# Branch gates of a hybrid mixer: eleven of twelve 256-column gate products of a Trainium2 encoder kernel made from seven half-size products

## The chip, the core and the metric

The kernel runs on one core of one Trainium2 chip. The metric is the device time of one execution in microseconds (us). A core has five engines with queues of their own: PE (TensorE, matrix products; PEld is its weight load), DVE (VectorE), ACT (ScalarE), POOL (GpSimd) and SP (SyncE, which issues the loads here). Each takes its instructions in the order of its queue and waits on semaphores for the others. Products are accumulated in PSUM, everything else lies in SBUF.

## The reference

One layer of an encoder over 512 positions of width 1024: a mixer with three gated branches, a cross attention into 256 memory tokens, a gated feed-forward block, and a last norm, all in fp32. The part that is changed is the end of the mixer:

```
p = h @ w_in                                   # h: 512 x 1024, norm of x
...                                            # ya, yb, yc: 512 x 512 each, from p's first columns
br_d = jnp.einsum("bsnc,ncd->bsnd", br, w_branch)     # br = [ya, yb, yc]
g = jax.nn.sigmoid(gates.reshape(bsz, seq, N_BRANCHES, D_MODEL))   # gates: p's last 3 x 1024 columns
merged = jnp.sum(g * br_d, axis=2)
return merged @ w_out
```

So for each of three branches there are a gate product (512 x 1024 by 1024 x 1024) and a branch product (512 x 512 by 512 x 1024).

## The kernel before

**Numbers.** Every fp32 operand of a product is cut into a part hi in the format fp32r (a cast on ACT) and a rest lo = x - hi (a subtraction on DVE); `split` (L101 to L109) and `cut` do both. A product is three accumulated ones: hi by hi, hi by lo, lo by hi. Activations are kept transposed, 128 channels on the partitions by 512 positions, as pairs: hT (the normed input, 8 blocks of 128 channels), ya, yb, yc (4 blocks each), mt (the merged sum, 8 blocks).

**Weights.** `load_raw` (L111) brings 1 MB of weights on SP's queue into one of three buffers (tag wr). `cut` makes pairs of 128 x 1024 elements from it in tags wh and wl, six buffers each (WB). `bank` (L86) hands out four PSUM banks in turn in this stage; the tag acc has four more.

**The gate stage (L660 to L692).** For each branch (yc, yb, ya, in this order) and each block d of 128 output channels, `col_gemm` makes the gate product (L674: 8 channel blocks by 3, so 24 matmuls that stream 512 columns), ACT takes the sigmoid out of PSUM (L676), `gemm` makes the branch product (L680: 12 matmuls of 512 columns), and DVE multiplies both (L683, L685). From the second branch on POOL adds the result to merged (L686); in the third branch `split` then cuts merged into mt (L688). Here Tile, the scheduler that orders the queues, is free: nothing is pinned. It takes instructions by the order of the program among those that its own timing has ready, so later work can fill an engine that it holds to be idle.

**Seven products (L225 to L348).** The feed-forward block already makes its products by Strassen-like sums: a product of (1024 x 256 weights) with (1024 x 512 activations), seen as 2 x 2 blocks, costs seven half-size block products in place of eight. The class `Seven` holds one such item: `sums` (two POOL operations, L242, L243) and `sums2` (two DVE operations, L248, L249) build the weights' sums, `hi` (ACT, L259) and `lo` (DVE, L264) cut them, `mul` (L272) makes one of the seven products (12 matmuls of 256 columns), `keep` (ACT, L278) copies an unfinished sum out of PSUM. The right factors are r11, r21, r22 (quarters of the activations) and t1 to t4 (their sums), which are made once. `seven_run` (L297) writes the order of one period out by hand: the products of item n, the last ones of its predecessor p, and the preparing of its successor q are interleaved:

```
PE:   l11 n, s1 n, s4 p, s2 n, l22 p, l12 n, s3 n
ACT:  u3 p, hi y n, m1 n, gate22 p, hi x q, hi s1 q, u2 n, done0 p, hi b q, c21 p
DVE:  c22 p, lo y n, lo x q, c12 p, sums2 q, lo s1 q, lo b q, c11 n
POOL: sums q
```

Here u3, m1 and u2 are the copies by `keep`; c11, c12, c22 are additions of a copy to what stands in PSUM (DVE, L942 in the feed-forward block); gate22, done0 and c21 finish an item. Each of these instructions is passed to `pin` (L225), which puts it behind the instruction that was written just before it for the same engine, whether that one is pinned or not. `seven_open` (L291) prepares the first item.

The feed-forward block uses this for its last 20 items (L989 to L999), with an item pair of gate and up product per 256 columns; its first 256 columns are made by `col_gemm` (L909 to L919).

**What follows the gate stage.** `Back` (L698) multiplies mt by w_out: `half0` goes through mt's blocks two by two for each of four row tiles (6 matmuls of 512 columns per step), with accumulators of the tag acc.

Of the kernel before, what the change touches and what calls it, by code (L numbers as in the profile page):

```python
# [8 lines left out]
F32 = mybir.dt.float32  # L9
# [8 lines left out]
def encoder_kernel(  # L18
# [39 lines left out]
    def close(p):  # L58
        p_close.pop(id(p))()
# [37 lines left out]
    def nm(s):  # L97
        uid[0] += 1
        return f"{s}{uid[0]}"

    def split(src, hi, lo, scale=None):  # L101

        if scale is None:
            nc.scalar.copy(out=hi, in_=src)  # L104
            nc.vector.tensor_tensor(out=lo, in0=src, in1=hi, op=ALU.subtract)  # L105
# [27 lines left out]
    def gemm(dst, lh, ll, rh, rl, ks, first=True, last=True):  # L133

        n, tot = 0, 3 * len(ks)
        for a, b in ((lh, rh), (lh, rl), (ll, rh)):
            for i, j in ks:
                nc.tensor.matmul(dst, a(i), b(j), start=first and n == 0, stop=last and n == tot - 1)  # L138
# [88 lines left out]
    class Seven:  # L227


        def __init__(self, src, fp, rights, tile_a):  # L230
            self.src, self.fp, self.r, self.tile_a = src, fp, rights, tile_a
            self.l = {}
# [41 lines left out]
                    n += 1  # L274

        def keep(self, name):
            m = self.fp.tile([P, 256], F32, name=nm(name), tag=name, bufs=1)
            pin(nc.scalar.copy(out=m, in_=self.a[:, 0:256]))  # L278
            return m

        def prepare(self):
# [6 lines left out]
            b = self.hi(("s2", "s4"), self.left)  # L288
            self.lo(b)

    def seven_open(items):  # L291
        items[0].load()
        items[0].sums()
        items[1].load()
        items[0].prepare()

    def seven_run(items):  # L297

        z = len(items)
        for k in range(z + 1):  # L300
            n = items[k] if k < z else None
            p = items[k - 1] if k else None
            q = items[k + 1] if k + 1 < z else None
            if k + 2 < z:
                items[k + 2].load()
            if n:
                n.a, n.c = n.tile_a(), n.tile_a()
                n.mul(n.a, "l11", "r11", True, False)
            if p:
# [24 lines left out]
            if p:  # L334
                p.done0()
                p.mul(p.a, "l22", "t4", False, True)
            if q:
                b = q.hi(("s2", "s4"), q.left)
            if p:
                p.c21(p.a[:, 0:256])  # L340
            if n:
                bk = bank(nm("pfb"))
                n.mul(bk, "l12", "r21", True, True)
            if q:
                q.lo(b)
            if n:
                n.c11(bk[:, 0:256], n.m1)
                n.mul(n.a, "s3", "t3", False, False)  # L348


    hp = pool("hp")
# [312 lines left out]
    for n, (b, y) in enumerate(((2, yc), (1, yb), (0, ya))):  # L664
        for half in range(2):
            gts = []
            for c in range(2):
                gts += w_cols(w_in, 8 * W + b * D + half * 512 + c * 256)
                if c == 0:
                    raw = load_raw(w_branch[b, :, half * 512:half * 512 + 512].rearrange("(k p) n -> p k n", p=P), CT, 512)  # L670
                for j in range(2):
                    d = 4 * half + 2 * c + j
                    pgt = bank(nm("pgt"))
                    col_gemm(pgt, gts[2 * c + j], hT, ALLT)  # L674
                    sg = gp.tile([P, T], F32, name=nm("sg"), tag="sg", bufs=3)
                    nc.scalar.activation(out=sg, in_=pgt, func=AF.Sigmoid)  # L676
                    if j == 0:
                        wb = cut(raw, (slice(None), slice(None), slice(c * 256, (c + 1) * 256)), CT, 256)
                    pbr = bank(nm("pbr"))
                    gemm(pbr, lambda i: wb[0][:, i, j * P:(j + 1) * P], lambda i: wb[1][:, i, j * P:(j + 1) * P],  # L680
                         lambda i: y[0][:, i, :], lambda i: y[1][:, i, :], [(i, i) for i in range(CT)])
                    if n == 0:
                        nc.vector.tensor_tensor(out=merged[:, d, :], in0=pbr, in1=sg, op=ALU.mult)  # L683
                    else:
                        nc.vector.tensor_tensor(out=sg, in0=pbr, in1=sg, op=ALU.mult)  # L685
                        nc.gpsimd.tensor_tensor(out=merged[:, d, :], in0=merged[:, d, :], in1=sg, op=ALU.add)  # L686
                        if n == 2:
                            split(merged[:, d, :], mt_[0][:, d, :], mt_[1][:, d, :])  # L688
    close(gp)
    close(yb_p)  # L690
    close(yp)
    close(hp)  # L692

# [210 lines left out]

    HT = (slice(0, T // 2), slice(T // 2, T))
    acc = lambda: psm.tile([P, 512], F32, name=nm("pf"), tag="acc", bufs=4)
    first = []  # L909
    for w in (w_gate_ffn, w_up_ffn):  # L910
        tiles = w_cols(w, 0)
# [24 lines left out]
    class Gate(Seven):  # L936
# [4 lines left out]
        def add(self, o, p, q):  # L941
            pin(nc.vector.tensor_tensor(out=o, in0=p, in1=q, op=ALU.add))  # L942
# [136 lines left out]
```

## Time and profile before

| | |
|---|---|
| median of three runs | 987.66 us (986.48 to 988.14) |
| the profiled execution's own time | 987.72 us |
| its span, first to last instruction | 986.0 us |
| mean granted TensorE clock | 0.994 |
| busy: PE, DVE, ACT, POOL | 964.4, 567.0, 433.2, 182.5 us |
| gate stage, 230.7 to 427.1 us | 196.4 us, PE busy 196.4 |
| seven products of the feed-forward block, 661.6 to 857.4 us | 195.8 us, PE busy 192.8 |

How to read it: the page gives each engine's busy time over the whole span; a row of a timeline gives start, length, engine, line of the kernel, operation, tiles written and read, shapes and count, and in brackets how long the engine sat idle before it and who released it. A row of the lines view gives a group with its busy time and the mean length of one in ns. A row of the windows view gives the busy time of each engine in a stretch, with the granted clock after PEclk.

### The profile page before, as it was taken

Reading aid. Unit: us, or ns where it says so; the run is one execution under the profiler, and the core shown is the slowest. Engines: PE = TensorE matmul, PEld = TensorE weight load, DVE = VectorE, ACT = ScalarE, POOL = GpSimd, SP = SyncE. Lnnn points to the kernel's source line nnn. Section 1 sums busy time; section 2 is a strip of 40 time slices with the busy share of each in tenths; the row PEclk is TensorE's granted clock in tenths of the full one; section 3 lists DMA queues with packets and bytes.
Section 4 is the critical chain, followed back from the end, with each engine's and each line's share of the span. In section 5 each row is a group of like instructions: output and inputs, shape, how many; then the busy total and the mean of one; then the engine's idle time right before and its main releaser. Section 6 shows DMA issues by size and latency. Waiting matters only on the chain. (4 is left out here: it accounts for less than half of the span.)

```text
span 986.0 us, 13484 instructions
## 1 busy us (share of the span) xinstructions
PE 964.4 (98%) x5546; PEld 847.5 (86%) x5546; DVE 567.0 (57%) x719; ACT 433.2 (44%) x652; POOL 182.5 (19%) x175
## 2 busy tenths in 40 slices
PE   7999999999999999999999999999999999899997
PEld 7988888887888888888988888899999999888885
DVE  6686888535323233436845545588888888762313
ACT  6464755334222223335735434554555555641301
POOL 1221123220001121220000000034454545100000
PEclk9999999999999999999999999999999999999999
DMA  9322222222313241362444121204233332532102
GB/s 296 132 86 71 70 74 89 73 86 86 128 43 128 87 128 44 133 211 81 172 153 146 55 74 44 66 21 129 89 126 112 104 128 87 187 107 93 63 1 85
DMA packets 77341, 100.76 MB, mean 102 GB/s; under 512 B 1904, under 2 KB 57248, under 8 KB 77280
## 3 DMA queue, kind: packets, MB, share of 16 engines
q1 hardware_dynamic: 76032, 95.45, 29.1%
q0 software_dynamic: 1248, 4.46, 1.2%
q8 instruction: 43, 0.70, 0.3%
q14 instruction: 18, 0.15, 0.0%
HBM read 97.80 MB, written 2.10 MB: 101 GB/s over the span
## 5 line engine op out<-in xcount | busy, mean ns | idle before, releaser
L105 DVE TENSOR_TENSOR wl<-wr,wh 128x1024 fp32r<-128x1024 f32 x134 | 164.8, 1236 | 204.6 <-ACT wh L104 129.8
L104 ACT CAST wh<-wr 128x1024 fp32r<-128x1024 f32 x134 | 139.8, 1051 | 224.1 <-PE pgt L138 81.1
L264 DVE TENSOR_TENSOR wl<-wr,wh 128x1024 fp32r<-128x1024 f32 x60 | 86.5, 1449 | 21.8 <-ACT wh L259 21.8
L166 POOL TENSOR_TENSOR rs<-ve,mhalf 128x1 f32<-128x1 f32 x22 | 16.0, 729 | 364.9 <-DVE ve L164 364.9
L259 ACT CAST wh<-wr 128x1024 fp32r<-128x1024 f32 x60 | 62.9, 1051 | 13.2 <-DVE wr L249 13.2
L686 POOL TENSOR_TENSOR merged<-merged,sg 128x512 f32<-128x512 f32 x16 | 27.7, 1728 | 184.4 <-DVE sg L685 184.4
L138 PE MATMUL pb<-wh,aTh 128*128 128x512 f32 x176 | 54.3, 390 | 1.7 <-ACT aTh L104 1.7
L138 PE MATMUL pb<-wl,aTh 128*128 128x512 f32 x176 | 54.3, 389 | 0.0
L138 PE MATMUL pb<-wh,aTl 128*128 128x512 f32 x176 | 53.7, 389 | 0.0
L138 PE MATMUL pgt<-hTh,wh 128*128 128x512 f32 x192 | 47.6, 390 | 1.1 <-DVE ybl L105 1.1
L138 PE MATMUL pgt<-hTl,wh 128*128 128x512 f32 x192 | 47.4, 389 | 0.0
L138 PE MATMUL pgt<-hTh,wl 128*128 128x512 f32 x192 | 47.4, 389 | 0.0
L278 ACT COPY u<-pf 128x256 f32<-128x256 f32 x40 | 14.9, 373 | 73.6 <-PE pf L272 71.2
L138 PEld LDWEIGHTS pgt<-hTh,wh 128*128 128x128 f32 x192 | 36.0, 188 | 8.7 <-DVE ybl L105 1.3
L243 POOL TENSOR_TENSOR wr<-wr 128x512 f32<-128x512 f32 x20 | 42.9, 2143 | 1.6
L138 PEld LDWEIGHTS pgt<-hTl,wh 128*128 128x128 f32 x192 | 36.0, 188 | 7.5
L138 PEld LDWEIGHTS pgt<-hTh,wl 128*128 128x128 f32 x192 | 36.0, 188 | 7.5
L138 PEld LDWEIGHTS pb<-wh,aTh 128*128 128x128 f32 x176 | 33.0, 188 | 8.7 <-ACT aTh L104 1.9
L242 POOL TENSOR_TENSOR s<-wr 128x512 f32<-128x512 f32 x20 | 26.1, 1304 | 72.2 <-DVE w L264 69.9
L138 PEld LDWEIGHTS pb<-wl,aTh 128*128 128x128 f32 x176 | 33.0, 188 | 6.9
L138 PEld LDWEIGHTS pb<-wh,aTl 128*128 128x128 f32 x176 | 33.0, 188 | 6.8
L544 POOL TENSOR_SCALAR_AFFINE_SELECT ab<-ab 128x128 f32<-128x128 f32 x32 | 23.8, 780 | 80.1 <-ACT ab L541 80.1
(271 smaller groups left out, 2205.5 us busy)
## 6 DMA issues: line engine op xcount, KB each, us to landing
wr<-in_w_in_dram SPq DMA_DIRECT2D x26, 1024.0 KB, 5.1
wr<-in_w_gate_ffn_dram SPq DMA_DIRECT2D x11, 1024.0 KB, 5.2
wr<-in_w_up_ffn_dram SPq DMA_DIRECT2D x11, 1024.0 KB, 5.6
wr<-in_w_down_ffn_dram SPq DMA_DIRECT2D x10, 1024.0 KB, 4.9
wr<-in_w_branch_dram SPq DMA_DIRECT2D x6, 1024.0 KB, 4.9
wr<-in_w_out_dram SPq DMA_DIRECT2D x4, 1024.0 KB, 5.0
wr<-in_w_k_xa_dram SPq DMA_DIRECT2D x4, 1024.0 KB
wr<-in_w_v_xa_dram SPq DMA_DIRECT2D x4, 1024.0 KB, 5.2
```

The lines of the kernel that those rows point to most:

```text
L104: nc.scalar.copy(out=hi, in_=src)
L105: nc.vector.tensor_tensor(out=lo, in0=src, in1=hi, op=ALU.subtract)
L138: nc.tensor.matmul(dst, a(i), b(j), start=first and n == 0, stop=last and n == tot - 1)
L166: nc.gpsimd.tensor_tensor(out=rs, in0=ve, in1=mhalf, op=ALU.pow)
L242: pin(nc.gpsimd.tensor_tensor(out=self.s1, in0=r[:, 0:4, P:256], in1=r[:, 4:8, P:256], op=ALU.add))
L243: pin(nc.gpsimd.tensor_tensor(out=r[:, 0:4, P:256], in0=r[:, 0:4, 0:P], in1=r[:, 0:4, P:256], op=ALU.subtract))
L259: pin(nc.scalar.copy(out=t[0], in_=src))
L264: pin(nc.vector.tensor_tensor(out=l, in0=src, in1=h, op=ALU.subtract))
L278: pin(nc.scalar.copy(out=m, in_=self.a[:, 0:256]))
L544: nc.gpsimd.affine_select(out=dg, in_=dg, compare_op=ALU.is_gt, fill=0.0, base=0, channel_multiplier=1, pattern=[[-1, P]])
L686: nc.gpsimd.tensor_tensor(out=merged[:, d, :], in0=merged[:, d, :], in1=sg, op=ALU.add)
```

## The change

The gates of eleven of the twelve items (an item is 256 gate columns of one branch) are made from seven half-size products. The first item keeps `col_gemm`; while it runs, the right factors t1 to t4 are made for the whole stage: hT's hi and lo are added again on POOL (8 operations on 128 x 512), the four sums are taken on DVE (16 operations on 128 x 256), and four `split`s cut them into the new pair hTt. The sums use the three weight buffers of the tag wr.

A new class `Branch` adds to `Seven` the branch product of its own 256 columns: `extra_load` brings 0.5 MB of w_branch into one buffer, `extra_cut` cuts it (ACT, DVE), `extra_mul` makes 24 matmuls of 512 columns and then multiplies, adds and splits as before. In `seven_run` the branch product of p comes after the last product of n. Multiplications and additions are pinned; the `split` of merged in the third branch is not, but it is written between pinned ones.

yc and yb move into pools on the right side, and mt takes their place once their last readers are through (from the ninth period on). The copies u3 and m1 now share one buffer (tag m) instead of one each, in the feed-forward block as well.

```diff
-            m = self.fp.tile([P, 256], F32, name=nm(name), tag=name, bufs=1)
+            m = self.fp.tile([P, 256], F32, name=nm(name), tag="u2" if name == "u2" else "m", bufs=1)
...
+            if k == at:
+                got = then()
             if k + 2 < z:
                 items[k + 2].load()
+            if n:
+                n.extra_load()
...
+            if p:
+                p.extra_cut()
             if n:
                 n.c11(bk[:, 0:256], n.m1)
                 n.mul(n.a, "s3", "t3", False, False)
+            if p:
+                p.extra_mul()
...
-    yc = tuple(yp.tile([P, CT, T], F32R, name=f"yc{s}") for s in "hl")
+    ycp = pool("ycp", side="right")
+    yc = tuple(ycp.tile([P, CT, T], F32R, name=f"yc{s}") for s in "hl")
...
-    yb_p = pool("ybp")
+    yb_p = pool("ybp", side="right")
...
-    mtp = pool("mtp", side="right")
-    mt_ = tuple(mtp.tile([P, KD, T], F32R, name=f"mt{s}") for s in "hl")
+    tp = pool("tp")
+    tp.tile([P, 48], F32, name="tpad")
+    hTt = tuple(tp.tile([P, 4, 4, T // 2], F32R, name=f"hTt{s}") for s in "hl")
...
+    gate2 = lambda: gp.tile([P, 2, T], F32, name=nm("sg"), tag="sg", bufs=2)
+    acc = lambda: psm.tile([P, 512], F32, name=nm("pf"), tag="acc", bufs=4)
+    class Branch(Seven):
...
+        def extra_load(self):
+            self.wraw = gp.tile([P, CT, 256], F32, name=nm("wb"), tag="wb", bufs=1)
+            nc.sync.dma_start(out=self.wraw, in_=self.wsrc)
+
+        def extra_cut(self):
+            t = [wp.tile([P, CT, 256], F32R, name=nm(f"w{s}"), tag=f"w{s}", bufs=WB) for s in "hl"]
+            pin(nc.scalar.copy(out=t[0], in_=self.wraw))
+            pin(nc.vector.tensor_tensor(out=t[1], in0=self.wraw, in1=t[0], op=ALU.subtract))
+            self.wb = t
+
+        def extra_mul(self):
+            y = self.y
+            for j in range(2):
+                d = self.d + j
+                pbr = bank(nm("pbr"))
+                m = 0
+                for w, v in ((0, 0), (0, 1), (1, 0)):
+                    for i in range(CT):
+                        pin(nc.tensor.matmul(pbr, self.wb[w][:, i, j * P:(j + 1) * P], y[v][:, i, :],
+                                             start=m == 0, stop=m == 3 * CT - 1))
+                        m += 1
+                sg = self.g[:, j, :]
+                if self.n == 0:
+                    pin(nc.vector.tensor_tensor(out=merged[:, d, :], in0=pbr, in1=sg, op=ALU.mult))
+                else:
+                    pin(nc.vector.tensor_tensor(out=sg, in0=pbr, in1=sg, op=ALU.mult))
+                    pin(nc.gpsimd.tensor_tensor(out=merged[:, d, :], in0=merged[:, d, :], in1=sg, op=ALU.add))
+                    if self.n == 2:
+                        split(merged[:, d, :], mt_[0][:, d, :], mt_[1][:, d, :])
...
+    it = Branch(0, 0)
+    it.extra_load()
+    gts = w_cols(w_in, 8 * W + BR[0][0] * D)
+    it.g = gate2()
+    for j in range(2):
+        pgt = bank(nm("pgt"))
+        col_gemm(pgt, gts[j], hT, ALLT)
+        nc.scalar.activation(out=it.g[:, j, :], in_=pgt, func=AF.Sigmoid)
+    for k in range(4):
+        f = wp.tile([P, 8, T // 2], F32, name=nm("wr"), tag="wr", bufs=3)
+        r11, r12, r21, r22, t1, t2, t3, t4 = (f[:, i, :] for i in range(8))
+        for i, kk in ((0, k), (2, k + 4)):
+            nc.gpsimd.tensor_tensor(out=f[:, i:i + 2, :], in0=hT[0][:, kk, :].rearrange("p (a b) -> p a b", a=2),
+                                    in1=hT[1][:, kk, :].rearrange("p (a b) -> p a b", a=2), op=ALU.add)
+        for o, a, b in ((t1, r12, r11), (t3, r22, r12), (t2, r22, t1), (t4, r21, t2)):
+            nc.vector.tensor_tensor(out=o, in0=a, in1=b, op=ALU.subtract)
+        split(f[:, 4:8, :], hTt[0][:, :, k, :], hTt[1][:, :, k, :])
+    it.extra_cut()
+    items = [Branch(n, c) for n in range(3) for c in range(4)][1:]
+    seven_open(items)
+    it.extra_mul()
...
+    def mt_open():
+        close(yb_p)
+        close(ycp)
+        p = pool("mtp", side="right")
+        mt_.extend(p.tile([P, KD, T], F32R, name=f"mt{s}") for s in "hl")
+        return p
+
+    mtp = seven_run(items, at=8, then=mt_open)
+    mt_ = tuple(mt_)
```

In `Branch` the methods c11, c22 and c12 are DVE additions into the gate's tile g, and gate22, done0 and c21 are sigmoids on ACT.

More of the change, by code (lines that the diff above doesn't have):

```diff
@@ L289, in prepare @@
             self.lo(b)
+        def extra_load(self):
+            pass
+        extra_cut = extra_mul = extra_load
     def seven_open(items):
@@ L295, in seven_open, with seven_run @@
         items[0].prepare()
-    def seven_run(items):
+    def seven_run(items, at=None, then=None):
         z = len(items)
@@ L348, in seven_run @@
                 n.mul(n.a, "s3", "t3", False, False)
+            if p:
+                p.extra_mul()
+        return got if then else None
     hp = pool("hp")
@@ L657, in encoder_kernel @@
     close(up)
-    mtp = pool("mtp", side="right")
-    mt_ = tuple(mtp.tile([P, KD, T], F32R, name=f"mt{s}") for s in "hl")
+    HT = (slice(0, T // 2), slice(T // 2, T))
+    tp = pool("tp")
+    tp.tile([P, 48], F32, name="tpad")
+    hTt = tuple(tp.tile([P, 4, 4, T // 2], F32R, name=f"hTt{s}") for s in "hl")
     gp = pool("gp")
     merged = gp.tile([P, KD, T], F32, name="merged")
[L664 to L688, printed above, removed]
@@ new lines, in encoder_kernel, with __init__, add, sig @@
+    gate2 = lambda: gp.tile([P, 2, T], F32, name=nm("sg"), tag="sg", bufs=2)
+    acc = lambda: psm.tile([P, 512], F32, name=nm("pf"), tag="acc", bufs=4)
+    BR = ((2, yc), (1, yb), (0, ya))
+    mt_ = []
+    class Branch(Seven):
+        def __init__(self, n, c):
+            b, self.y = BR[n]
+            c0 = 8 * W + b * D + c * 256
+            super().__init__(w_in[:, c0:c0 + 256], gp, rights, acc)
+            self.n, self.d = n, 2 * c
+            self.wsrc = w_branch[b, :, c * 256:(c + 1) * 256].rearrange("(k p) n -> p k n", p=P)
+        def add(self, o, p, q):
+            pin(nc.vector.tensor_tensor(out=o, in0=p, in1=q, op=ALU.add))
+        def sig(self, o, i):
+            pin(nc.scalar.activation(out=o, in_=i, func=AF.Sigmoid))
+        def c11(self, p, m):
+            self.g = gate2()
+            self.add(self.g[:, 0, HT[0]], p, m)
+        def c22(self, p, m):
+            self.add(self.g[:, 1, HT[1]], p, m)
+        def gate22(self):
+            self.sig(self.g[:, 1, HT[1]], self.g[:, 1, HT[1]])
+        def c12(self, p, m):
+            self.add(self.g[:, 0, HT[1]], p, m)
+        def done0(self):
+            self.sig(self.g[:, 0, :], self.g[:, 0, :])
+        def c21(self, p):
+            self.sig(self.g[:, 1, HT[0]], p)
+        def extra_load(self):
+            self.wraw = gp.tile([P, CT, 256], F32, name=nm("wb"), tag="wb", bufs=1)
[24 more added lines that the diff above has]
+                        split(merged[:, d, :], mt_[0][:, d, :], mt_[1][:, d, :])
@@ new lines, in encoder_kernel @@
+    rights = dict(r11=tuple(v[:, 0:4, HT[0]] for v in hT), r21=tuple(v[:, 4:8, HT[0]] for v in hT),
+                  r22=tuple(v[:, 4:8, HT[1]] for v in hT))
+    for i in range(4):
+        rights[f"t{i + 1}"] = tuple(v[:, i] for v in hTt)
+    it = Branch(0, 0)
[6 more added lines that the diff above has]
+        nc.scalar.activation(out=it.g[:, j, :], in_=pgt, func=AF.Sigmoid)
@@ L689, in encoder_kernel @@
+    it.extra_cut()
[10 more added lines that the diff above has]
+    mt_ = tuple(mt_)
     close(gp)
-    close(yb_p)
+    close(tp)
     close(yp)
@@ L903, in encoder_kernel @@
     bx.half1(lambda t: t > 0 and norm_turn3(t - 1))
-    HT = (slice(0, T // 2), slice(T // 2, T))
-    acc = lambda: psm.tile([P, 512], F32, name=nm("pf"), tag="acc", bufs=4)
     first = []
```

## The prediction

> **What bounds the kernel now.** I read the page first, then the windows of two stages, then the timeline around them.
>
> ```profile
> span 986.0 us, 13484 instructions
> ...
> PE 964.4 (98%) x5546; PEld 847.5 (86%) x5546; DVE 567.0 (57%) x719; ACT 433.2 (44%) x652; POOL 182.5 (19%) x175
> ...
> PE 31%; DVE 2%; ACT 1%; issue 1%; DVEq 0%; POOLq 0%; POOL 0%; ACTq 0%
> ```
>
> PE is busy for 98% of the span and leads the chain that ended last. The windows compare the stage that is changed with the one that already runs the seven products:
>
> ```profile
> 230.70:427.10 196.40, 196.40 (x867) 162.67 (x868) 64.49 (x69) 57.84 (x68) 27.72 (x19) 1.00 0.30 99
> 661.60:857.40 195.80, 192.84 (x1683) 192.25 (x1681) 161.52 (x192) 105.67 (x174) 88.39 (x58) 0.99 0.36 117
> ```
>
> The columns are length, then busy time of PE, PEld, DVE, ACT, POOL. In the gate stage PE never stops and DVE works a third of the time. In the other, DVE is at 161.5 of 195.8. So PE's work is what the gate stage costs, and the change trades it for DVE, ACT and POOL work that is now pinned.
>
> **What it removes.** A streamed matmul's price is the distance of starts:
>
> ```profile
> 238.95 1.98 PE L138 MATMUL pgt<-hTh,wh 128*128 128x512 f32 x8
> ...
> 255.27 1.98 PE L138 MATMUL pgt<-hTh,wh 128*128 128x512 f32 x8
> ...
> 701.29 0.62 PE L272 MATMUL pf<-h3l,wh 128*128 128x256 f32 x4
> ...
> 708.10 0.62 PE L272 MATMUL pfb<-h3l,wh 128*128 128x256 f32 x4
> ```
>
> Between the first two lie two gate blocks and two branch blocks, 72 matmuls in 16.32 us: 0.2267 us for 512 columns. Between the last two lie 15 groups of four, 6.81 us: 0.1135 us for 256, exactly half. An item's gates cost 48 x 0.2267 = 10.88 us now and 7 x 12 x 0.1135 = 9.53 us after. Eleven items: 11 x 1.35 = **14.8 us less**. The branch products stay, 24 x 0.2267 = 5.44 us an item. A period is then 15.0 us, if nothing waits.
>
> **What a period costs the others.** Durations:
>
> ```profile
> L264 DVE TENSOR_TENSOR wl<-wr,wh 128x1024 fp32r<-128x1024 f32 x60 | 86.5, 1449 | 21.8 <-ACT wh L259 21.8
> L259 ACT CAST wh<-wr 128x1024 fp32r<-128x1024 f32 x60 | 62.9, 1051 | 13.2 <-DVE wr L249 13.2
> L243 POOL TENSOR_TENSOR wr<-wr 128x512 f32<-128x512 f32 x20 | 42.9, 2143 | 1.6
> L242 POOL TENSOR_TENSOR s<-wr 128x512 f32<-128x512 f32 x20 | 26.1, 1304 | 72.2 <-DVE w L264 69.9
> L249 DVE TENSOR_TENSOR wr<-wr 128x512 f32<-128x512 f32 x20 | 22.6, 1130 | 0.7
> L248 DVE TENSOR_TENSOR wr<-s,wr 128x512 f32<-128x512 f32 x20 | 13.6, 682 | 0.1
> L685 DVE TENSOR_TENSOR sg<-pbr,sg 128x512 f32<-128x512 f32 x16 | 11.1, 691 | 24.0 <-PE pbr L138 24.0
> L942 DVE TENSOR_TENSOR g<-pf,u 128x256 f32<-128x256 f32 x20 | 8.3, 414 | 0.9 <-ACT u L278 0.5 <-PE pf L272 0.3
> ```
>
> DVE: four lo cuts (three of the gates, one of the branch) 4 x 1.45, the small one and the two sums 0.68 + 0.68 + 1.13, three additions 1.24, two multiplications 1.38: 10.9 us, and 1.4 more where merged is split. ACT, with four casts of 1.05, the small one, three copies and the sigmoids, has less. That fits in 15.0, so the average binds nothing. The order does. Means hide one thing:
>
> ```profile
> 313.27 1.22 DVE L105 TENSOR_TENSOR wl<-wr,wh 128x1024 fp32r<-128x1024 f32 x1
> 313.43 2.20 POOL L686 TENSOR_TENSOR merged<-merged,sg 128x512 f32<-128x512 f32 x1 [6.87 <-DVE sg L685]
> ...
> 708.53 1.29 POOL L242 TENSOR_TENSOR s<-wr 128x512 f32<-128x512 f32 x1 [1.23 <-DVE w L264]
> ...
> 708.97 1.93 DVE L264 TENSOR_TENSOR wl<-wr,wh 128x1024 fp32r<-128x1024 f32 x1 [0.19 <-ACT wh L259]
> ...
> 709.90 2.17 POOL L243 TENSOR_TENSOR wr<-wr 128x512 f32<-128x512 f32 x1
> ```
>
> A POOL operation of 512 elements takes 1.29 us alone and a lo cut 1.22. Whichever starts second while the other runs ends about as late as if it had waited: 1.29 + 0.9, 1.22 + 0.7. I therefore let a POOL operation and a DVE operation with two SBUF inputs run one after the other.
>
> **Middle periods: 4 x 1.0 us.** From the second branch on POOL must add, and the next item's sums are pinned behind that. Count from the end of a branch product. First two rows on how fast a product is picked up:
>
> ```profile
> 426.63 0.62 PE L138 MATMUL pb<-wh,mth 128*128 128x512 f32 x2
> ...
> 426.90 0.69 DVE L685 TENSOR_TENSOR sg<-pbr,sg 128x512 f32<-128x512 f32 x1 [1.51 <-PE pbr L138]
> ```
>
> Multiplication 0.27 to 0.95; POOL's addition to 2.4; a lo cut that waited for it to 3.5; POOL's first sum to 4.6; the next lo cut to 5.7; second sum to 6.9; sums2 0.68 + 0.69 to 8.2; hi b 1.05 to 9.3; ACT's sigmoid c21 (0.39, below) to 9.55; the branch weights' cast 1.05 to 10.5. PE has done its seven products at 9.53 and waits 1.0 us for that cast. This holds for the four periods that follow an addition without a split; in the first branch the sums aren't behind an addition and there is slack. Bounds: 0 (cuts and sums side by side: 2.2 less) to 2 x 4 (each operation at its longest). I take 4.1.
>
> ```profile
> L104 ACT CAST mth<-merged x8: 620/622/622, 371.9 to 429.9; 128x512 fp32r<-128x512 f32 x8
> L105 DVE TENSOR_TENSOR mtl<-merged,mth x8: 691/692/693, 372.5 to 430.6; 128x512 fp32r<-128x512 f32 x8
> ...
> 717.78 0.39 ACT L945 ACTIVATE g<-pf 128x256 f32<-128x256 f32 x1
> ```
>
> **Third branch: 4.9 us.** The split is written between pinned instructions. So DVE's second multiplication stands behind the first block's lo, which needs POOL's addition and ACT's cast: from the first block's end (2.72 before the period's end) 0.27 + 0.69 + 1.29 + 0.62 + 0.69 = 3.6, and with the steps from engine to engine (an estimate, 0.1) 1.0 after the end. Then 0.69, addition 1.3, cast 0.62, lo 0.69, and only then c22 (0.42), because it is pinned behind that lo, as the copy u3 is behind the cast: 4.8 to 5.3. s4 of PE, the third product, needs c22 and could start at 2 x 1.36 = 2.72. PE waits 2.1 us, 2.6 where a sum of POOL falls in between. Two such periods and 0.1 behind: 4.9 (4 to 6).
>
> **The last period: 1.0 us.** The last item's s4 has nothing before it on PE: 4.8 us, and 1.6 for the cast later, 6.4. The first steps of w_out can fill it if the scheduler puts them there: two accumulators are free and two pairs of mt blocks are done, 2 x 2 x 6 x 0.2267 = 5.4. That leaves 1.0, at most 6.4.
>
> **The start: 3.0 us.**
>
> ```profile
> 222.74 3.50 DVE L105 TENSOR_TENSOR wl<-wr,wh 128x1024 fp32r<-128x1024 f32 x3 [9.29 <-ACT wh L104]
> ...
> 229.92 2.48 DVE L105 TENSOR_TENSOR ybl<-pgt,ybh 128x512 fp32r<-128x512 f32 x4
> ...
> 230.66 2.11 PE L138 MATMUL pgt<-hTh,wh 128*128 128x512 f32 x8 [1.07 <-DVE ybl L105]
> ```
>
> The first item gives PE 16.3 us from 230.66. In that time DVE has, after ybl, the 16 subtractions (0.34 each, half of L248's), four lo cuts, the branch's, and the first item's lo cuts and sums: 5.4 + 4.9 + 1.2 + 5.2 = 16.7 us from 232.4, so 2 us late. DVE sat idle 9.29 us before 222.74, so part can run ahead, as far as weight buffers allow. I take 1 (0 to 3). Then the first period has no branch products: PE needs 6.8 us, while DVE prepares the next item in about as much and waits for POOL's sums: 2.0 (the feed-forward block's own start has 1.89, next fence).
>
> **Clock: 1.7 us.**
>
> ```profile
> 673.26 0.74 PE L272 MATMUL pf<-h3h,wh 128*128 128x256 f32 x4 [1.89 <-DVE g L942]
> ...
> 674.75:678.20 3.45, 3.45 (x19) 3.45 (x18) 3.36 (x6) 0.98 (x3) 0.00 (x0) 0.51 0.62 195
> ```
>
> After 1.89 us without work the granted clock was 0.51 for about 3.4 us, which costs half of that. The waits of 2.1 and 2.6 are longer; the 1.07 above had no such effect. I count one of them. The Trainium skill ("TensorE: Matmul & The Clock Gate", Why this matters for your kernels) has the clock drop after gaps of over some 3 us; by that rule nothing drops here and the sum is 1.7 lower. The trace does not agree: 1.89 us were enough.
>
> **One buffer for u3 and m1: 0.5 us.** Now u3 must wait for the previous c11:
>
> ```profile
> 701.10 0.37 ACT L278 COPY u<-pf 128x256 f32<-128x256 f32 x1 [1.96 <-PE pf L272]
> ...
> 710.62 0.37 ACT L278 COPY u<-pf 128x256 f32<-128x256 f32 x1 [1.68 <-PE pf L272]
> 710.82 0.41 DVE L942 TENSOR_TENSOR g<-pfb,m 128x256 f32<-128x256 f32 x1
> ...
> 713.08 0.62 PE L272 MATMUL pf<-h3h,wh 128*128 128x256 f32 x4
> ```
>
> In every second period u3 moves from 710.62 to 711.25. c22 then ends at 712.1; its product starts at 713.08, so the move is covered. At the block's start the 1.89 grows by about 0.5.
>
> **The sum.** -14.8 + 4.1 + 4.9 + 1.0 + 3.0 + 1.7 + 0.5 = +0.4 us. The profiled execution's own time is 987.72 (span 986.0 and 1.7 around it), 0.06 over the median of the runs shown. Forecast: 988.1, no change that a measurement can tell; 0.2% is 2.0 us, about what it can tell.
>
> At nothing I cost: the mt pool on the right (mt's first half lies on yc, its second on yb, read for the last time a period earlier); the w_branch loads (0.5 MB, issued some 13 us before their cast); POOL's loads of x, which come when hT is free and stand before work that has 16 us of w_out products as cover. Without that cover each costs at most its own 0.6 to 2 us.
>
> **Rivals.**
> 1. *The waits stay covered* (faster). DVE and POOL find an order without the 4.1, the factors are ready in time, no clock drop, the other 0.5 absent: -14.8 + 2.0 + 4.3 + 1.0 = -7.5, 980.2. For it: a third of DVE is idle in a period; against it: the order is written out and the operations get in each other's way in every period. 0.24.
> 2. *The clock holds*: gaps of 2 to 3 us cost no more than themselves, as that of 1.07 did; 1.7 less than forecast, 986.4. Against it speaks the row with 0.51. 0.08. (This is the case that the Trainium skill's page named above describes.)
> 3. *The last period stays open* (slower). The queue of PE gets no w_out step before the last s4, or w_out's weight pairs take two of the six wh buffers and hold up a pinned cast: 5.4 more and one more clock drop, 988.1 + 7.1 = 995.2. It decides once PE idles over 4 us before that product. For it: four accumulators are taken until just before; against it: the scheduler fills PE by readiness. 0.20.
> 4. *The shared buffer binds the feed-forward block* (slower). From u3 at 701.10 to the end of the next c11 at 711.23 are 10.1 us, and the same chain in the other kind of period, counted by its operations, is 9.0: 19.15 for a pair against 19.07 of PE. With 0.4 us more a pair the last nine pairs lose 3.6: 991.7. 0.08.
> That the products do not get cheaper I leave without a chance: the 256-column rows are of the same shape, and their weight loads are hidden there.
>
> **How the numbers follow.** Forecast 0.40, with its own range 985.5 to 991 (faster 0.07, same 0.20, slower 0.13, from the bounds of the start, the middle and the clock). Rival 1 is faster, 0.24. Rival 2: same 0.06, faster 0.02. Rival 3: slower 0.20. Rival 4: slower 0.07, same 0.01. Faster 0.33, same 0.27, slower 0.40. The range runs from rival 1 to rival 3, 979.5 to 995.5; beyond it lie all bounds at one end.
>
> **What would show it.** In the changed kernel's windows the gate stage should last about 196 us again, with PE busy some 181 to 184 in it. The waits view should have PE waiting for ACT's cast of the branch weights four times by about 1 us, and for DVE's c22 twice by 2 to 3 us late in the stage. Matmuls of w_out should stand before the last item's s4. A stage of under 190 us would show that the waits were covered and make the forecast wrong; so would a stage near 196 whose waits stand elsewhere, for the reasons. The feed-forward block should stay at 195.8 to 197.

## The result, and the profile after

The changed kernel takes 1000.47 us (median of 11 runs) against 988.06 before. The ratio is 1.010, 95% interval 1.0069 to 1.0131: slower by about 1%. The forecast was 988.1, its range ended at 995.5. The ratio leaves out one run of 5059.93 us of the changed kernel, whose others took 996.07 to 1003.7, and one of 1076.97 of before, whose others lie in two groups, near 987.7 and near 994.3, which widens every interval here.

The profiled execution took 1000.47 us, with a span of 998.7 against 986.0. First the page of after, in the lines that answer to those of before:

```profile
span 998.7 us, 14466 instructions
...
PE 963.6 (96%) x5942; PEld 864.2 (87%) x5942; DVE 649.2 (65%) x816; ACT 460.7 (46%) x722; POOL 233.6 (23%) x205
```

PE is busy for as long as before (964.4), although eleven items were to take 14.8 us off it, and it stands still for 13.5 us more. So two things went wrong: waits, and products that cost more than they should.

The windows say where. First from the first gate product to the end of the w_out products, before and then after (the edges are PE's: 230.66 is the first gate matmul of before, 474.08 the first matmul behind w_out); the third row is the feed-forward block of after, which took 197.37 us before:

```profile
230.66:474.08 243.42, 243.42 (x1092) 201.98 (x1093) 89.49 (x110) 83.55 (x116) 34.10 (x27) 1.00 0.31 104
```

```profile
228.10:482.80 254.70, 239.21 (x1485) 214.69 (x1486) 164.89 (x199) 116.18 (x192) 73.72 (x51) 0.98 0.34 114
671.10:871.70 200.60, 195.97 (x1683) 194.65 (x1681) 165.35 (x193) 106.41 (x176) 88.64 (x58) 1.00 0.36 116
```

The stage starts 2.6 us earlier and lasts 11.3 longer, the feed-forward block 3.2 longer, and 0.8 lies between the two: 12.7 in all. In the stage PE waits 254.70 - 239.21 = 15.5 us, where it had not waited at all. The waits view of after names them (waited for: total, times, longest, in us):

```profile
PE pf L272 <- DVE sg L697: 9.6, 4, 4.5
...
PE pbr L739 <- ACT wh L727: 4.0, 5, 1.4
...
PE pbr L739 <- DVE wl L728: 1.9, 2, 1.0
```

L697 holds the additions c11, c22 and c12, L727 is the cast of the branch weights, L728 their lo cut. The timeline of PE in after puts each at its place; the bracket is the wait before the row:

```profile
257.18 0.74 PE L272 MATMUL pf<-hTh,wh 128*128 128x256 f32 x4 [1.24 <-DVE sg L697]
...
327.80 0.50 PE L739 MATMUL pbr<-ybh,wh 128*128 128x512 f32 x1 [0.64 <-ACT wh L727]
...
387.15 0.74 PE L272 MATMUL pf<-hTh,wh 128*128 128x256 f32 x4 [2.14 <-DVE sg L697]
...
405.98 0.74 PE L272 MATMUL pf<-hTh,wh 128*128 128x256 f32 x4 [1.71 <-DVE sg L697]
...
423.19 1.22 PE L272 MATMUL pf<-hTh,wh 128*128 128x256 f32 x4 [4.52 <-DVE sg L697]
...
430.08 1.20 PE L739 MATMUL pbr<-yah,wh 128*128 128x512 f32 x4 [1.41 <-ACT wh L727]
...
432.03 1.98 PE L138 MATMUL pb<-wh,mth 128*128 128x512 f32 x8
```

The wait of 0.64 comes four times (327.80 to 376.43). 4.52 stands before the last item's s4, and the first matmul of w_out, which was to fill that wait, starts at 432.03, behind it; before it there is none.

What happens in those 4.52 us is the split of the third branch between two pinned rows. The timeline of all engines in after, from the end of the branch product before (its last row of POOL is 416.76, the addition of the first block):

```profile
418.08 0.62 ACT L104 CAST mth<-merged 128x512 fp32r<-128x512 f32 x1 [6.31 <-POOL merged L747]
...
418.73 0.69 DVE L105 TENSOR_TENSOR mtl<-merged,mth 128x512 fp32r<-128x512 f32 x1 [2.05 <-ACT mth L104]
419.34 0.68 DVE L746 TENSOR_TENSOR sg<-pbr,sg 128x512 f32<-128x512 f32 x1
420.17 1.26 POOL L747 TENSOR_TENSOR merged<-merged,sg 128x512 f32<-128x512 f32 x1 [2.12 <-DVE sg L746]
421.46 0.62 ACT L104 CAST mth<-merged 128x512 fp32r<-128x512 f32 x1 [2.76 <-POOL merged L747]
...
422.11 0.69 DVE L105 TENSOR_TENSOR mtl<-merged,mth 128x512 fp32r<-128x512 f32 x1 [2.09 <-ACT mth L104]
422.72 0.42 DVE L697 TENSOR_TENSOR sg<-pf,u 128x256 f32<-128x256 f32 x1
```

Six steps in a row, each waiting for the one before, and c22 (L697) at the end, which needs none of them: it is only queued behind the lo of the second block. Two stretches of after also ran at half the granted clock (windows; the clock stands third from the end):

```profile
388.40:391.80 3.40, 3.40 (x18) 3.40 (x17) 3.37 (x6) 1.00 (x3) 0.00 (x0) 0.50 0.42 126
...
422.50:429.30 6.80, 5.49 (x24) 5.19 (x24) 1.06 (x3) 1.63 (x4) 2.20 (x4) 0.50 0.17 66
```

Half of PE's 3.40 + 5.49 us, 4.4 us, is an estimate of what that lost.

The last part is in no wait. In these rows the spacing changes with the streamed tile (timeline of after, starts of groups of four matmuls of 256 columns):

```profile
393.00 0.63 PE L272 MATMUL pfb<-hTh,wh 128*128 128x256 f32 x4
...
394.42 0.64 PE L272 MATMUL pf<-hTth,wh 128*128 128x256 f32 x4
394.89 0.62 PE L272 MATMUL pf<-hTtl,wh 128*128 128x256 f32 x4
395.35 0.62 PE L272 MATMUL pf<-hTth,wl 128*128 128x256 f32 x4
```

From 393.00 to 394.42, with hT streamed, twelve take 1.42 us, 0.118 each; from 394.89 to 395.35, with hTt, four take 0.46, 0.115 (the group between, at the change from one to the other, takes 0.47). The forecast's price was 0.1135. Over the whole stage the mean is 0.1170 (some 870 of the 924, those not at half clock or beside a wait), which makes 924 x 0.0035 = 3.2 us.

### The profile page after: what moved, and what is told of

It is laid out like the page before. It is cut to its first block, busy times and chain, and to the rows that moved or that the text cites. A ratio compares the mean times of both kernels' runs of the same rounds, so it can differ in the third digit from the quotient of the medians.

```text
span 998.7 us, 14466 instructions
## 1 busy us (share of the span) xinstructions
PE 963.6 (96%) x5942; PEld 864.2 (87%) x5942; DVE 649.2 (65%) x816; ACT 460.7 (46%) x722; POOL 233.6 (23%) x205
## 5 line engine op out<-in xcount | busy, mean ns | idle before, releaser
L105 DVE TENSOR_TENSOR wl<-wr,wh 128x1024 fp32r<-128x1024 f32 x100 | 124.3, 1252 | 115.5 <-ACT wh L104 89.6
L264 DVE TENSOR_TENSOR wl<-wr,wh 128x1024 fp32r<-128x1024 f32 x93 | 140.7, 1525 | 31.0 <-ACT wh L259 31.0
L278 ACT COPY u<-pf 128x256 f32<-128x256 f32 x62 | 23.1, 373 | 107.3 <-PE pf L272 32.2
L242 POOL TENSOR_TENSOR s<-wr 128x512 f32<-128x512 f32 x31 | 44.4, 1432 | 118.7 <-DVE w L264 114.5
L243 POOL TENSOR_TENSOR wr<-wr 128x512 f32<-128x512 f32 x31 | 65.8, 2124 | 2.4
L830 DVE TENSOR_TENSOR xr<-pb,xr 128x512 f32<-128x512 f32 x24 | 16.1, 687 | 34.3 <-PE pb L138 33.9
L272 PE MATMUL pf<-h3th,wh 128*128 128x256 f32 x240 | 37.5, 278 | 0.0
L272 PE MATMUL pf<-h3tl,wh 128*128 128x256 f32 x240 | 37.5, 278 | 0.0
L272 PE MATMUL pf<-h3th,wl 128*128 128x256 f32 x240 | 37.5, 278 | 0.0
L175 ACT ACTIVATE jk<-xr 128x512 f32<-128x512 f32 x24 | 15.1, 631 | 46.3 <-DVE xr L830 46.0
L1066 POOL TENSOR_TENSOR af<-af,g 128x256 f32<-128x256 f32 (+1 forms) x20 | 23.1, 1156 | 42.9 <-DVE af L1039 42.9
```

Of the source, the lines that this page charges most:

```text
L242: pin(nc.gpsimd.tensor_tensor(out=self.s1, in0=r[:, 0:4, P:256], in1=r[:, 4:8, P:256], op=ALU.add))
L243: pin(nc.gpsimd.tensor_tensor(out=r[:, 0:4, P:256], in0=r[:, 0:4, 0:P], in1=r[:, 0:4, P:256], op=ALU.subtract))
L264: pin(nc.vector.tensor_tensor(out=l, in0=src, in1=h, op=ALU.subtract))
L272: pin(nc.tensor.matmul(dst[:, 0:256], w[:, k, :], v[:, k, :], start=first and n == 0, stop=last and n == 11, skip_group_check=True))
L1066: pin(eng.tensor_tensor(out=o, in0=o if p is None else p, in1=self.gate.g[:, j, cs], op=ALU.mult))
```

## The experiments

Theory: the split between pinned rows makes the three waits before s4 and, with them, the half clock; pinned places farther back remove it without any product being moved, and the middle waits go if either the additions or the cast change places. Rivals: the empty PE queue at the end of the stage is the cause (no w_out steps there); the shared buffer of u3 and m1 makes the feed-forward block slower; the spacing of the matmuls comes from where their tiles lie.

**e1_split_late: the split of merged a period later.**

```diff
                     pin(nc.gpsimd.tensor_tensor(out=merged[:, d, :], in0=merged[:, d, :], in1=sg, op=ALU.add))
-                    if self.n == 2:
-                        split(merged[:, d, :], mt_[0][:, d, :], mt_[1][:, d, :])
+
+        def late(self):
+            if self.n == 2:
+                for d in range(self.d, self.d + 2):
+                    split(merged[:, d, :], mt_[0][:, d, :], mt_[1][:, d, :])
...
                 p.c12(p.c[:, 0:256], p.u2)
+            if k > 1:
+                items[k - 2].late()
...
                 p.extra_mul()
+        items[z - 1].late()
```

> The third branch's split of merged is written one period later, behind the addition c12 of the next item, so that no pinned multiplication, addition or copy stands behind it. Theory (the split between pinned instructions makes the late waits, these halve the clock, and the last period stays open because of it): the waits of 2.14, 1.71 and 4.52 us before s4 in the last three periods shrink to 0, 0 and about 1.4, the two stretches at half clock (5.8 us together in the profile of the change) go, and the span falls by some 11 to 14 us from 998.7 to 985 to 988. Rival (PE lacks other operands there, the split only happens to stand beside it): the waits move to another releaser and the span stays above 994.

Measured: 989.95 us, ratio to before 1.0003 (0.9977 to 1.0028), where the change itself had 1.010. The profiled execution took longer, 993.78 us with a span of 992.1, above the 985 to 988 that were expected: its feed-forward block ran at the slower spacing that the last section shows. Its stage lasts 245.80 us in place of 254.70 (windows, then the timeline's last three waits of PE in this run):

```profile
228.00:473.80 245.80, 235.89 (x1491) 211.18 (x1490) 169.87 (x199) 116.71 (x193) 75.70 (x51) 1.00 0.36 118
```

```profile
394.51 1.19 PE L742 MATMUL pbr<-yah,wh 128*128 128x512 f32 x4 [1.48 <-ACT wh L730]
...
416.64 0.74 PE L272 MATMUL pf<-hTh,wh 128*128 128x256 f32 x4 [1.12 <-DVE sg L700]
...
421.12 1.19 PE L742 MATMUL pbr<-yah,wh 128*128 128x512 f32 x4 [1.41 <-ACT wh L730]
```

The waits of 2.14 and 1.71 are gone and 4.52 has become 1.12, with no w_out step before it; the clock stays at 1.00 (the two stretches at 0.50 in after are 10.2 us long by their windows, not the 5.8 of the expectation). So 8.9 us of the stage hang on the place of the split. A new wait of 1.48 has come at 394.51, for the same cast as in the middle periods: DVE now has mt's two lo cuts (0.68 us each alone) ahead of c12 and the sums (the split is not pinned, and the scheduler queued it ahead of the addition behind which it is written), so hi b and the cast behind it come later. The queue of PE that was empty at the end is not needed to explain the 4.5; filling it would have hidden it.

**e5_add_late and e6_cut_early: two ways past the middle waits.** Both start from e1. In e5 POOL's additions, too, come a period later, behind the sums; in e6 the cast and the cut of the branch weights come ahead of hi b.

```diff
                 q.sums()
+            if k > 1:
+                items[k - 2].late_add()
```

```diff
                 p.mul(p.a, "l22", "t4", False, True)
+            if p:
+                p.extra_cut()
             if q:
...
                 q.lo(b)
-            if p:
-                p.extra_cut()
             if n:
```

> As with the split written late, and POOL's additions to merged are also written one period later, behind the sums of the next item. Theory (the sums wait behind the addition, and the cast of the branch weights stands behind their chain): the four waits of 0.64 us before the branch products of the second branch (0.91 from start to start with the slowed matmul) and the one of 1.48 go, the gate stage gets 4 to 5 us shorter than with the late split alone. Rival (DVE is simply too busy in these periods): the waits stay or move to the branch product's lo part.

> As with the split written late, and the cut of the branch weights is written ahead of hi b, which waits for the sums; POOL's additions stay where they are. Theory (the cast is late only because it is queued on ACT behind hi b): the four waits of 0.64 us and the one of 1.48 go here too, 4 to 5 us; in the last period the 1.41 before the branch product shrinks. Rival (POOL and DVE together are late, wherever the cast stands): the waits move to the second product s4 or to s2 of the next period, and the stage is as long.

Measured: e5 983.6 us, ratio 0.9947 (0.9921 to 0.9972); e6 981.77, ratio 0.992 (0.9887 to 0.9952). Their stages last 239.71 and 237.45 us, 6.1 and 8.4 less than e1's where 4 to 5 were expected; PE's waits account for 4.2 and 5.6 of that. The second branch's product, which waited 0.64 in after, follows its predecessor without a wait in both (timelines of PE, e5 and then e6; no bracket):

```profile
326.63 0.62 PE L272 MATMUL pf<-hTth,wl 128*128 128x256 f32 x4
327.09 1.08 PE L745 MATMUL pbr<-ybh,wh 128*128 128x512 f32 x4
```

```profile
323.80 0.62 PE L272 MATMUL pf<-hTth,wl 128*128 128x256 f32 x4
324.25 1.08 PE L742 MATMUL pbr<-ybh,wh 128*128 128x512 f32 x4
```

The chain of the forecast (hi b behind the sums, the sums behind the addition, the branch's cast behind hi b) is shown by both: cut either link and the wait is gone. e1's 1.48 went with it in both, and in e6 the last period's 1.41 shrank to 0.74.

**e2_m_apart and e4_before_m: the shared buffer.** e2 is the changed kernel with u3 and m1 apart in the feed-forward block; e4 is the kernel before with one buffer for both.

```diff
+        apart = True
...
-            m = self.fp.tile([P, 256], F32, name=nm(name), tag="u2" if name == "u2" else "m", bufs=1)
+            m = self.fp.tile([P, 256], F32, name=nm(name), tag=name if self.apart or name == "u2" else "m", bufs=1)
...
     class Branch(Seven):
+        apart = False
```

> u3 and m1 get a buffer each again in the feed-forward block alone; the gates keep the shared one. Theory (the shared buffer delays DVE's chain there): the feed-forward stage, 200.6 us from its first of seven products to w_down's first matmul, falls to 197 to 198, the total by about 2 to 3 us. Rival (the stage is longer because PE itself streams 256 columns in 0.118 us instead of 0.113 from 780 us on, which the buffer has no part in): the stage stays at 199 to 201 or changes with the run, whatever the buffer.

> The kernel before with one change: u3 and m1 share a buffer, so only the feed-forward block is touched. Theory (the shared buffer costs the block 0.5 us at its start and little else): 988 to 989 against 987.7. Rival (the chain through the shared buffer is longer than PE's two periods): the block loses 0.2 to 0.4 us a pair, 3 us or more in all, and 990 to 992.

Measured: e2 995.45 us, ratio 1.0069 (1.004 to 1.0098); e4 990.85, ratio 1.0016 (0.9989 to 1.0043). Their feed-forward blocks, in the windows (e2, then e4):

```profile
667.44:863.27 195.83, 191.22 (x1683) 190.63 (x1681) 163.88 (x193) 107.46 (x176) 88.66 (x58) 1.00 0.37 119
```

```profile
663.30:862.06 198.76, 194.04 (x1682) 192.88 (x1680) 164.40 (x193) 106.47 (x176) 88.65 (x58) 0.99 0.37 117
```

e4's block is 198.76 - 197.37 = 1.4 us longer than that of before. Its 990.85 lies in the range of its rival, not of its theory, but the interval does not tell the two apart. The traces show that the rival's chain exists. In after, c11 (L1039) frees the shared buffer, the copy u3 waits for it, c22 (L1039 too) waits for u3, and s4 starts about 0.1 us late (timeline; the bracket of 2.42 is ACT's):

```profile
778.12 0.41 DVE L1039 TENSOR_TENSOR g<-pfb,m 128x256 f32<-128x256 f32 x1
778.64 0.37 ACT L278 COPY u<-pf 128x256 f32<-128x256 f32 x1 [2.42 <-DVE g L1039]
778.97 0.62 PE L272 MATMUL pf<-h3th,w 128*128 128x256 f32 x4
779.05 0.42 DVE L1039 TENSOR_TENSOR g<-pf,u 128x256 f32<-128x256 f32 x1 [0.52 <-ACT u L278]
779.53 0.74 PE L272 MATMUL pf<-h3h,wh 128*128 128x256 f32 x4
```

From 778.97 to 779.53 four matmuls take 0.56 in place of 0.45, and the first matmul behind (0.74 in place of 0.62) costs another 0.1. The waits view does not show this, because the rows of PE overlap (0.62 long, 0.45 apart). It recurs every second period, at 702.47, 721.74, 741.00, 760.26 and 779.53 in after, 19.27 us apart where PE alone needs 19.07: 0.2 us a pair, 1.1 in all. e4 has it four times (from 772.45 on, 0.9 in all), e3, e5 and e6 have it too; e1, where PE itself is slower nearly throughout, does not, and neither does any block with two buffers (before, e2, e7, e8). So rival 4 had the chain right; the 3.6 us is not there, since it came in five pairs at most and at 0.2, not 0.4. The rest of the 4.8 us between the blocks of after and e2 is the spacing: e2's matmuls stood at 0.113 until 858.51, after's at 0.118 up to the wait that ends at 683.20 and again from 779.53 on. Whether the buffer has a part in that is open (last section). e2's three waits before s4 were still 2.14, 1.71 and 4.52.

**e3_align: other offsets.** By the addresses of the built kernel, the product that streams hT with weights of tag wh finds both tiles at 32 bytes past a multiple of 128; hTt with the small pair w has both at 96. Where the two differ, by 64, in after (hTt with wh) and in the feed-forward block, the spacing can be 0.1135. e3 moves hT and hTt by pads so that no pair of them agrees.

```diff
     hp = pool("hp")
+    hp.tile([P, 48], F32, name="hTpad")
...
     tp = pool("tp")
-    tp.tile([P, 48], F32, name="tpad")
...
     gp = pool("gp")
+    gp.tile([P, 16], F32, name="gpad")
```

> Three pads move hT, its sums and the small weight pair w2, so that in each of the seven gate products the streamed tile and the weight tile start 64 bytes apart modulo 128, as they do in the feed-forward block; before, r11, r21 and r22 and the product with s1 start at the same offset. Nothing else is changed. Theory (matmuls of 256 columns whose two operands start at the same offset modulo 128 bytes are spaced by 0.119 us, others by 0.1133): the spacing is 0.113 to 0.114 in all seven gate products, the gate stage is 3 to 4 us shorter, and the V products at the start, whose offsets also part, gain about 1 us. Rival (the spacing follows from the waits or from DVE and ACT traffic): spacing and stage stay as they are.

Measured: 1001.0 us, ratio 1.0107 (1.0068 to 1.0147): no gain. For most of the stage all its products stood at 0.118, whatever they streamed, and not at the expected 0.113. Only the V products at the start (26 to 45 us), whose offsets part too, went down, from 0.1198 to 0.1178. What this leaves over is taken up with e8.

**e7_all_unaligned and e8_all: the three moves and the buffer together.** e7 is e1, e5, e6 and, in the feed-forward block, e2 in one kernel. e8 is e7 with e3's pads. Nothing else is edited.

> Late split, late additions, early cut, and u3 and m1 apart in the feed-forward block. Theory: of the 20 us of waits and half clock in the gate stage only the start (some 3 us) and about 1 us in the last period are left; the gate stage, from its first matmul to the first K product, is 237 to 240 us against 243.4 before and 254.7 in the change; total 981 to 984 against 987.7, if the feed-forward block streams at 0.113.

> The same with the three pads that part the streamed and the weight tiles by 64 bytes modulo 128. Theory (same offset makes 0.119 us): 3 to 4 us less than without the pads, 978 to 981. Rival (the slower spacing is a state of PE that comes and goes, as in the feed-forward block, and the offset has no part in it): the same time as without the pads, and stretches at 0.118 in products whose offsets differ.

Measured: e7 979.2 us (976.93 to 979.85), ratio 0.9883 (0.9847 to 0.9919): it beats both kernels. e8 981.63 (979.11 to 989.02), ratio 0.994 (0.991 to 0.997). The windows of e7, stage and feed-forward block:

```profile
228.27:465.27 237.00, 232.77 (x1484) 210.54 (x1485) 168.12 (x199) 115.08 (x192) 72.69 (x51) 1.00 0.37 123
...
653.21:850.57 197.36, 192.75 (x1682) 192.16 (x1681) 163.72 (x193) 107.35 (x176) 87.93 (x58) 0.99 0.37 118
```

The first row closes the account of the stage to within 1.0 us: 243.42 before, less 14.8 for the products, plus waits of 4.2 (237.00 - 232.77), plus 3.2 for the spacing (mean 0.1170 here too), is 236.0; 237.0 was measured. e7's total is below the expected 981 to 984, e8's above its 978 to 981.

The pads' effect can be seen, but only in places (e8's timeline, early and late in the stage; starts of groups of four):

```profile
247.39 0.64 PE L272 MATMUL pf<-hTh,wh 128*128 128x256 f32 x4
...
249.74 0.64 PE L272 MATMUL pf<-hTth,w 128*128 128x256 f32 x4
...
393.62 0.62 PE L272 MATMUL pf<-hTh,wh 128*128 128x256 f32 x4
...
395.89 0.62 PE L272 MATMUL pf<-hTth,w 128*128 128x256 f32 x4
```

Five groups lie between the first two and between the last two: 2.35 us for 20 matmuls, 0.1175, and 2.27, 0.1135. The same kinds of product stand 3.5% farther apart at 250 than at 394. In e7, without the pads, those that stream hT had a mean of 0.119 over the stage (394 matmuls) and never fell to 0.1135 for a whole group. So agreeing offsets went with 0.119, and with differing ones there are still two spacings. Means over the stage, from the starts in the traces, show why the pads bring nothing: from e7 to e8, hT's products went from 0.1190 to 0.1167 and those of hTt with the small pair from 0.1179 to 0.1170, but those of hTt with wh and wl, whose offsets differ in both kernels, went up from 0.1145 to 0.1164. The offset is thus not the only cause. What switches between the two stays open, and e8 is no faster than e7.

## Why the prediction was wrong

The forecast had the stage change by -0.1 us, the start of it included; it grew by 11.3. Term by term:

**Products, -14.8: right, but not at that price.** Every number of matmuls was right. The row of 0.1135 was one of the feed-forward block, and I took it for a constant of 256 columns. In the new place the mean was 0.1170: 3.2 us given back. This term was put at nothing ("the 256-column rows are of the same shape"), although the trace of before holds another price for that shape, in the K products of the cross attention (timeline of before):

```profile
476.39 1.12 PE L138 MATMUL pk<-mTl,wh 128*128 128x256 f32 x8
477.35 1.12 PE L138 MATMUL pk<-mTh,wl 128*128 128x256 f32 x8
```

Eight matmuls in 0.96 us are 0.120 each.

**Middle periods, 4.1: right in cause, smaller.** Four waits for the cast of the branch weights, at 0.64 us by the trace, 2.6 in all. e5 and e6 show the chain.

**Third branch, 4.9: right in cause, 1.0 smaller.** The waits before s4 are 2.14 and 1.71, 3.9, and the chain is the predicted one row by row, as shown for the last period (418.08 to 422.72). e1 shows that the place of the split makes it.

**The last period, 1.0: the step that failed.** "The first steps of w_out can fill it if the scheduler puts them there" was an assumption with no row behind it. It put the first of them, eight matmuls at 432.03, behind the last s4, so PE waited 4.52 and 1.41, 5.9 together, 4.9 more than the sum had. Unfilled, these waits were put at 4.8 and 1.6, close to what came: the wait was right, the filling of it was not. It was rival 3, at 0.20 and 995.2. Why the scheduler took the steps of w_out no earlier was not tried and stays open.

**Start, 3.0: right.** Waits of 1.00 in the first item, then 1.24 and 0.90, 3.1. Not foreseen was that the stage begins 2.6 us earlier: before, PE waited 0.84 and 1.07 for DVE ahead of the first gate product, and in after, where the scheduler ordered the rows ahead of the stage differently, it did not wait. That is 1.9 of the 2.6.

**Clock, 1.7: mis-sized, 4.4.** One window was counted. The wait of 2.14 gave one of 3.4 us, and 4.52 one of 6.8. The Trainium skill ("TensorE: Matmul & The Clock Gate", Why this matters for your kernels) has the throughput drop after idle gaps of more than some 3 us. 4.52 us agrees; 2.14 doesn't, in this run. What the traces have in its place is in the last section.

**The shared buffer, 0.5: too small.** The prediction moved u3 once and found the move covered; carried on from pair to pair it is not: the late starts of s4 cost 1.1 us in after and 0.9 in e4, and the wait at the block's start grew by 0.2 (2.05 against 1.89), not 0.5.

Waits of 15.5 against 13.0 in the sum (2.5), the clock (2.7 more), the spacing (3.2) make 8.4 of the 11.4 that the stage is off. A product behind a wait takes longer to get going, too: rows of 0.74 and 1.20 in place of 0.62 and 1.07, about 0.12 for each of the eleven, 1.3. Some 1.7 us stay unassigned. Outside the stage the earlier start gives 2.6 back, and the feed-forward block takes 3.2: 3.7 for the spacing (mean 0.1156 over 1680 products against 0.1134 before), 1.1 for the late starts and 0.2 for the longer wait, less the 1.7 that before's block lost at half clock (674.75 to 678.20) and after's did not.

The forecast's sign rested on terms that nearly cancel, +0.4 in all; two of them were taken at the lower end of their bounds (the last period, 1.0 with "at most 6.4", and the clock, one window of 1.7 where the two waits before s4 and an open last period could each have made one). With both at the other end it would have been 988.1 + 5.4 + 3.4 = 996.9, still 3.6 below the 1000.47 that was measured.

## What to carry to other kernels

In an order written out by hand, look for the unpinned operation between two pinned ones: whatever is pinned behind it inherits its waits, here a chain of six steps in front of an addition that needed none of them; 8.9 us went when it was written a period later. A wait that "the scheduler will fill" is to be counted in full until a row of the trace shows the filling work ahead of it in the queue. And the price of a matmul is to be taken with a margin when tiles move, even for the same shape: 0.113 to 0.120 us for 256 columns here.

## What the runs showed of the hardware

**Two spacings of one matmul.** Products of 256 columns stood at 0.113 or at 0.118 us in the same execution, on tiles of the same names. The feed-forward block of after shows the switch (timeline, groups of four; the first pair lies ahead of it, the second behind):

```profile
777.15 0.62 PE L272 MATMUL pf<-h3l,wh 128*128 128x256 f32 x4
777.61 0.62 PE L272 MATMUL pf<-h3h,wl 128*128 128x256 f32 x4
...
780.57 0.63 PE L272 MATMUL pf<-h3h,wl 128*128 128x256 f32 x4
781.04 0.64 PE L272 MATMUL pf<-h3th,wh 128*128 128x256 f32 x4
```

The slower spacing lasted there to the end of the block; in e1 from 673.90 to the end (block 203.3 us long), in e3 from 819.54 to the end, in e6 from 683.90 to 850.50 (202.7), in e4 only up to the wait that ends at 675.42. before, e5, e7 and e8 had none of it and e2 had it only from 858.51 on, for its last 5 us. A block nearly all at 0.118 is some 7 us longer than one at 0.113 (203.3 in e1, 195.83 in e2).

In these blocks each switch stands right behind a wait or a late start of PE, at 683.20 and 779.53 in after and at the times just given for the others. At 779.53 (after), 819.54 (e3) and 683.90 (e6) it is the late start of s4 that the shared buffer makes. Most late starts switch nothing (702.47 to 760.26 in after), and e5 shares the buffer and stood at 0.113, so sharing it is not enough. But the four blocks with two buffers had next to nothing of the slower spacing, and five of the six that share it had more: that the buffer has no part in it is not shown either.

**What halved the clock was not the length of a wait alone.** e7's wait of 1.89 us was followed by 0.50, e8's of 1.90 by 1.00; the 2.14 of after by 0.50, the same wait of e2 by 1.00; e3's 2.52 by 0.50, e1's 2.51 by 1.00. What tells them apart is where they lie in time. Within each of the ten traces the granted clock changes only at times that are whole multiples of 3.413 us apart. Cut into stretches of that length, e7 and e8 look like this around those waits (windows, e7 and then e8; what PE's busy time leaves of the 3.41 us is its wait):

```profile
662.15:665.56 3.41, 1.52 (x13) 1.32 (x12) 3.41 (x4) 2.21 (x5) 2.96 (x2) 1.00 0.18 59
665.56:668.97 3.41, 3.41 (x18) 3.41 (x17) 3.38 (x5) 1.09 (x2) 0.00 (x0) 0.50 0.39 123
```

```profile
664.37:667.78 3.41, 1.60 (x14) 1.60 (x15) 3.41 (x5) 2.21 (x5) 2.14 (x2) 1.00 0.00 1
667.78:671.19 3.41, 3.41 (x33) 3.41 (x32) 3.25 (x5) 1.87 (x4) 0.04 (x1) 1.00 0.68 213
```

e7's wait lies in one stretch with all its 1.89 us, e8's with 1.81; the other 0.08 lies in the stretch before. Between 20 and 970 us the ten traces have ten stretches in which PE stood still for 1.89 us or more, and the next one was at 0.50 each time. No other stretch at 1.00 was followed by one at 0.50. e2's 2.14 is divided into 0.57 and 1.57, e1's 2.51 into 1.35 and 1.16. The clock then stayed at 0.50 for 3.41 us, and for 6.83 after the 4.5 us wait in all three kernels that have it (after, e2, e3). Where the stretches begin differs from trace to trace, so a wait of about 2 us is worth 2 us or 3.7, and its length does not say which.
